# Both MLP products of an encoder block by Strassen's algorithm, with activations and residual rows passed through DRAM

## The chip, the cores and the metric

The kernel runs on one core of a Trainium2 chip. The metric is device time in microseconds of one execution; three runs of the kernel before have a median of 2367.69 us. The profile is one execution on the chip, and its times are in microseconds from the first instruction. The engines are TensorE (PE; its weight loads are PEld), VectorE (DVE), ScalarE (ACT), GpSimd (POOL) and SyncE (SP), which here only issues transfers.

## The reference

One layer of a streaming encoder for 512 tokens of width 2048, in f32: a norm, an input projection, latent attention and sparse attention side by side, an output projection, cross attention to 256 memory tokens, and then the part that this case is about:

```python
        x = x + memory_cross_attention(hc, mem_n, ...)     # ends with the product by w_o_cross
        hm = rmsnorm(x, g_mlp[l])
        x = x + jnp.square(jax.nn.relu(hm @ w_up[l])) @ w_down[l]     # 2048 -> 8192 -> 2048
    return rmsnorm(x, g_final)
```

## The kernel before

Activations lie feature-major: a tile has 128 features on the partitions and the 512 tokens along the free axis. Each f32 operand of a product is taken apart into two float32r halves, hi and lo, and a product of two tiles is three matmuls into the same PSUM bank: hi x hi, hi x lo, lo x hi (`fmm3`, matmuls at L292).

The program is one stream of *units*. A unit is a block of weights, 128 x 1024 f32 (512 KB), with the products made from it. `loader` sends its DMA on SyncE's queue into one of three `wraw` buffers, `splitter` takes it apart (`hi_lo`: ScalarE casts the block to `whi`, VectorE subtracts, `wlo = wraw - whi`), three units ahead at most, and `unit.pe` issues the matmuls. All instructions of ScalarE, VectorE and GpSimd go through a helper at L134, so the profile gives that line for nearly all of them; they are told apart by tile and shape. The order of each engine's instructions is settled while the program is written out: background tasks (Python generators) yield the time at which they can go on, and a plan with a clock for each engine (`Plan`, `Planned._cost`) decides when a task's next instruction is given to its engine. On the chip each engine runs its own list in order and waits at its head.

The MLP goes through the 8192 hidden features in eight chunks `c`. For a chunk, 16 up units make eight tiles of 128 hidden features: 16 contraction tiles, each product 128 x 512 into one of eight banks. When a bank is complete, `relu2` multiplies it by the tokens' norm `bc` (VectorE), applies relu and square (VectorE) and splits it into two `slot` tiles `A2` (ScalarE, VectorE). Then 16 down units multiply these tiles and `add_down` adds each finished bank to the residual `res[n]`, which stays on chip all along. The last eight down units (`last_units`) keep their weights on chip and run over the tokens in two halves of 256, so that the first half's final norm and store (`gen_out`) lie beside the second half's products. Ahead of the MLP, the eight units of `w_oc` finish the cross attention; `residual` adds each bank to the residual, writes its gained halves `NEWX` and sums its squares on GpSimd.

Matmuls of the MLP before: 248 units of 24 over 512 columns, and 8 units of 48 over 256 columns.

## Time and profile before

| what | value |
|---|---|
| median of three runs | 2367.69 us (2367.07 to 2368.04) |
| span of the profiled execution | 2365.2 us |
| TensorE busy in it | 2329.9 us, 99% |
| VectorE, ScalarE, GpSimd busy | 1123.1, 744.5, 173.0 us |
| moved by DMA | 234.91 MB, mean 99 GB/s |

The span runs from the first to the last instruction; the run's time contains it and some 2.5 us around it. A matmul's record is longer than the distance to the next one's start, because matmuls are pipelined: the pace is read from start to start, not from the record's length. Records of VectorE overlap a little in the same way.

### The profile page before, as it was taken

The numbers are of one execution on the slowest core, as the hardware profiler recorded it, in microseconds if no ns is written. First come the engines' busy times: TensorE is split into PE (matmuls) and PEld (weight loads), VectorE is DVE, ScalarE is ACT, GpSimd is POOL, SyncE is SP. The second block draws the span as 40 slices with busy tenths as digits, with TensorE's granted clock in tenths as the row PEclk, the third lists the DMA queues.
The fourth block names the chain that finished last, engine by engine and source line by source line (L and its number), as shares of the span: only waits on it lengthen the run. The fifth ranks groups of instructions, "written<-read, shape, count | busy, mean of one in ns | idle before, by whom it ended". The sixth has DMA issues, their size and how long they took to land.

```text
span 2365.2 us, 28572 instructions
## 1 busy us (share of the span) xinstructions
PE 2329.9 (99%) x11608; PEld 2020.0 (85%) x11608; DVE 1123.1 (47%) x1769; ACT 744.5 (31%) x1145; POOL 173.0 (7%) x232
## 2 busy tenths in 40 slices
...
GB/s 171 102 87 94 67 78 84 65 108 40 92 165 96 169 113 120 91 97 98 98 98 98 98 93 95 97 98 98 98 98 96 93 96 98 98 98 98 98 96 92
DMA packets 74406, 234.91 MB, mean 99 GB/s; under 512 B 8193, under 2 KB 12305, under 8 KB 74017
## 3 DMA queue, kind: packets, MB, share of 16 engines
...
## 4 chain that ended last, share of the span: by engine, by line
PE 59%; DVE 0%; POOL 0%; issue 0%; DVEq 0%; ACT 0%; POOLq 0%; ACTq 0%
PE bank L292 59%; DVE fb L134 0%; POOL fb L134 0%; PE bank L311 0%; DVEq L1719 0%; ACT fb L134 0%; POOL small L134 0%; POOLq L134 0%; ACTq L134 0%
## 5 line engine op out<-in xcount | busy, mean ns | idle before, releaser
L292 PE MATMUL bank<-slot,whi 128*128 128x512 f32 x4452 | 1382.3, 389 | 0.0
L134 DVE TENSOR_TENSOR wlo<-wraw,whi 128x1024 fp32r<-128x1024 f32 (+4 forms) x434 | 502.7, 1158 | 1064.9 <-ACT whi L134 1063.9
L292 PEld LDWEIGHTS bank<-slot,whi 128*128 128x128 f32 x4452 | 834.9, 188 | 171.5
L292 PE MATMUL bank<-slot,wlo 128*128 128x512 f32 x2268 | 883.2, 389 | 0.0
L134 ACT CAST whi<-wraw 128x1024 fp32r<-128x1024 f32 (+4 forms) x434 | 427.6, 985 | 1289.3 <-PE bank L292 1249.4
L292 PEld LDWEIGHTS bank<-slot,wlo 128*128 128x128 f32 x2268 | 425.8, 188 | 87.8
L292 PE MATMUL bank<-whi,slot 128*128 128x384 f32 (+4 forms) x1944 | 487.9, 329 | 7.4 <-ACT slot L134 6.9
L292 PEld LDWEIGHTS bank<-whi,slot 128*128 128x128 f32 x1944 | 343.5, 189 | 14.5 <-ACT slot L134 6.9
L292 PE MATMUL bank<-wlo,slot 128*128 128x384 f32 (+4 forms) x972 | 319.3, 329 | 0.5 <-DVE wlo L134 0.5
L134 POOL TENSOR_TENSOR fb<-fb 128x512 f32<-128x512 f32 (+5 forms) x118 | 108.3, 928 | 1668.9 <-issue 1348.2
L292 PEld LDWEIGHTS bank<-wlo,slot 128*128 128x128 f32 x972 | 184.0, 189 | 4.2 <-DVE wlo L134 0.9
L134 DVE TENSOR_TENSOR fb<-fb,bank 128x512 f32<-128x512 f32 (+1 forms) x192 | 122.5, 640 | 63.2 <-PE bank L292 61.8
L292 PE MATMUL bank<-slot,slot 128*128 128x256 f32 (+2 forms) x677 | 127.9, 311 | 0.6 <-DVE ptb L134 0.4
L292 PE MATMUL bank<-ptb,whi 128*128 128x512 f32 x380 | 123.8, 389 | 0.0
L292 PEld LDWEIGHTS bank<-slot,slot 128*128 128x128 f32 x677 | 103.3, 190 | 6.6 <-DVE slot L134 0.9
L292 PEld LDWEIGHTS bank<-ptb,whi 128*128 128x128 f32 x380 | 71.3, 188 | 14.8
L134 ACT CAST slot<-fb 128x512 fp32r<-128x512 f32 x75 | 46.2, 621 | 73.7 <-DVE fb L134 73.6
L311 PE MATMUL bank<-cs,fb 128*128 128x128 f32 x384 | 60.2, 275 | 9.0 <-POOL fb L134 3.6
L292 PE MATMUL bank<-ptb,slot 128*128 128x256 f32 (+1 forms) x323 | 65.3, 308 | 1.5 <-ACT slot L134 0.9
L134 DVE SCALAR_TENSOR_TENSOR slot<-fb,gn,slot 128x512 fp32r<-128x512 f32 (+1 forms) x75 | 65.4, 896 | 1.1 <-ACT slot L134 0.7
L134 ACT ACTIVATE fb<-fb 128x512 f32<-128x512 f32 (+2 forms) x94 | 51.1, 551 | 39.0 <-DVE fb L134 34.8
L311 PEld LDWEIGHTS bank<-cs,fb 128*128 128x128 f32 x384 | 46.3, 140 | 17.3 <-POOL fb L134 5.8
...
## 6 DMA issues: line engine op xcount, KB each, us to landing
wraw<-in_w_up_dram SPq DMA_DIRECT2D x128, 512.0 KB, 3.3
wraw<-in_w_dn_dram SPq DMA_DIRECT2D x128, 512.0 KB, 3.3
...
wraw<-in_w_out_dram SPq DMA_DIRECT2D x32, 512.0 KB, 3.3
fb<-in_xT_dram SPq DMA_DIRECT2D x16, 256.0 KB, 4.2
wraw<-in_w_in_dram SPq DMA_DIRECT2D x16, 256.0 KB, 2.6
fb<-in_xT_dram SPq DMA_DIRECT2D x8, 512.0 KB, 6.0
fb<-in_memT_dram SPq DMA_DIRECT2D x16, 256.0 KB, 3.1
```

What stands on the lines that cost most here:

```text
L134: r = fn(*args, **kw)
L292: nc.tensor.matmul(out, lhsT, rhs, start=start, stop=stop)
L311: nc.tensor.transpose(out, in_, ident)
```

## The change

The up and the down product are each cut into blocks of two by two (features, contraction, and token halves of 256) and made by the form of Strassen's algorithm with seven block products in place of eight. What goes with it:

- `strassen_split`: a unit's weights are four blocks of 256 columns. GpSimd forms four sums of them into a ring of two buffers (`sring`), then three blocks as they are (768 columns) and the four sums (1024 columns) are cast and subtracted into one of two buffers `HI`, `LO`.
- `strassen_pe`: a unit makes seven products of 256 columns for two feature halves `e`, three matmuls each. Seven banks stay open over the eight units of a group; the eighth is free.
- For the right-hand side four sums are needed too. `gen_xpair` makes them once for the eight pairs of input tiles, on VectorE for the first two pairs and on GpSimd for the others, and keeps pairs in `big`. For the hidden activations, `gen_up_out` combines the seven banks of an up group into four blocks (`c11`, `c21`, `c12`, `c22`), applies relu, square and the squared norm, forms the sums and both halves (`HT`, `G`), and ScalarE's queue stores them to `tp_dram`.
- All 16 up groups (8 units each) run first, then 16 down groups: four contraction quarters `c`, four output groups `ng`. `gen_load_t` loads the pairs of a quarter on ScalarE's queue into the place of a pair whose last product is issued.
- `residual1` stores the residual rows to `xs_dram`; `gen_load_res` loads them, on SyncE's queue, into the space of `G`, `HT` and `CT` when the last up group has been stored. `gen_down_out` adds the seven banks of a down group to them, the parts on PSUM by VectorE, the others by GpSimd (by VectorE for the last group).
- The two-half end is gone: `gen_square` sums squares by group, and `gen_out` scales and stores all 16 tiles after the last product.
- The plan has other costs for the MLP, and some buffers share one tile.

```diff
...
-    whi = [cp.tile([128, 1024], F32R, name=f"whi{i}") for i in range(3)]
-    wlo = [cp.tile([128, 1024], F32R, name=f"wlo{i}") for i in range(3)]
...
+    hl = cp.tile([128, 2 * PAIR], F32R, name="hl")
+    whi = [hl[:, 2048 * i : 2048 * i + 1024] for i in range(3)]
+    wlo = [hl[:, 2048 * i + 1024 : 2048 * i + 2048] for i in range(3)]
...
+    xs_dram = nc.dram_tensor("xs_dram", (KT, 128, 512), F32, kind="Internal").ap()
+    tp_dram = nc.dram_tensor("tp_dram", (32, 128, PAIR), F32, kind="Internal").ap()
...
+    def smm(out, lhsT, rhs, start, stop):
+        nc.tensor.matmul(out, lhsT, rhs, start=start, stop=stop, skip_group_check=True)
+        plan.issue("pe", 13.4 + rhs.shape[-1] / 2.4, [out], [lhsT, rhs], 30)
+        step()
...
                             fmm3(st[i], w_block(h, l, j, i), koper(k), k == 0, k == nk - 1)
                         if kk == nk // 2 - 1:
-                            spawn(residual(phase, 4 * ng + i, st[i], gain), True)
...
+    def residual1(n, b):
+        yield rt(b, res[n])
+        dve.tensor_tensor(res[n], res[n], b, op=OP.add)
+        banks_f.put(b)
+        flag.add(("x1", n))
+        if n % 2:
+            spawn(gen_xpair(n // 2), True)
+        yield rt(res[n])
+        nc.sync.dma_start(xs_dram[n], res[n])
+        while n > 0 and ("sq", 1, n - 1) not in flag:
+            yield 0
+        if n == 0:
+            act.activation(acc_r, res[n], AF.Square)
+        else:
+            act.activation(sq_r[n % 2], res[n], AF.Square)
+            yield rt(sq_r[n % 2])
+            pool.tensor_tensor(acc_r, acc_r, sq_r[n % 2], op=OP.add)
+        flag.add(("sq", 1, n))
+    def sums(dst, b12, b11, b21, b22, eng):
+        t1, t2, t3, t4 = dst
+        eng.tensor_tensor(t3, b22, b12, op=OP.subtract)
+        eng.tensor_tensor(t1, b12, b11, op=OP.subtract)
+        eng.tensor_tensor(t2, t3, b11, op=OP.add)
+        eng.tensor_tensor(t4, t2, b21, op=OP.subtract)
+    def gen_xpair(q):
+        while ("x1", 2 * q) not in flag or ("x1", 2 * q + 1) not in flag:
+            yield 0
+        gx = (yield from take(gxbufs))[0]
+        x1, x2 = res[2 * q], res[2 * q + 1]
+        g1, g2 = (g_mlp[:, 2 * q + j : 2 * q + j + 1] for j in range(2))
+        yield rt(x1, x2)
+        act.activation(gx[:, 0:256], x1[:, 256:512], AF.Copy, scale=g1)
+        act.activation(gx[:, 512:1024], x2, AF.Copy, scale=g2)
+        act.activation(gx[:, 256:512], x1[:, 0:256], AF.Copy, scale=g1)
+        yield rt(gx)
+        c = lambda i: gx[:, 256 * i : 256 * i + 256]
+        sums([c(4), c(5), c(6), c(7)], c(0), c(1), c(2), c(3), dve if q < 2 else pool)
+        pr = yield from take_pair(q)
+        for a, n in ((0, 768), (768, 1024)):
+            src = gx[:, 256 + a : 256 + a + n]
+            yield from hi_lo(pr[:, a : a + n], pr[:, 1792 + a : 1792 + a + n], src)
+        gxbufs.put(gx)
+        XP[q] = pr
+        flag.add(("xp", q))
+        if q == 3:
+            while not all(("sq", 1, n) in flag for n in range(8)):
+                yield 0
+            gxbufs.put(fslot(6144, 2048))
...
+    def strassen_split(i):
+        raw, s = wraw[i % 3], sring[i % 2]
+        hi, lo = HI[units[i].buf], LO[units[i].buf]
+        while i == first_s and not all(("xp", q) in flag and ("sq", 1, 2 * q + 1) in flag for q in range(2)):
+            yield 0
+        while not splits[i - 2].done:
+            yield 0
+        yield rt(raw)
+        two = lambda x: x.rearrange("p (u c) -> p u c", u=2)
+        a21 = raw[:, 0:256]
+        pool.tensor_tensor(two(s[:, 0:512]), two(raw[:, 256:768]), a21.unsqueeze(1).to_broadcast([128, 2, 256]), op=OP.add)
+        pool.tensor_tensor(s[:, 512:768], s[:, 256:512], raw[:, 256:512], op=OP.add)
+        pool.tensor_tensor(s[:, 768:1024], s[:, 512:768], raw[:, 768:1024], op=OP.add)
+        while ("pe", i - 2) not in flag:
+            yield 0
+        yield from hi_lo(hi[:, 0:768], lo[:, 0:768], raw[:, 256:1024])
+        yield from hi_lo(hi[:, 768:1792], lo[:, 768:1792], s)
+    def strassen_pe(buf, st, pair, first, last, order):
+        hi, lo = HI[buf], LO[buf]
+        for r in order:
+            w, t = PRODUCTS[r]
+            if first:
+                st[r] = take_now(banks_f)[0]
+            th, tl = pair[:, 256 * t : 256 * t + 256], pair[:, 1792 + 256 * t : 2048 + 256 * t]
+            for e in range(2):
+                out = st[r][:, 256 * e : 256 * e + 256]
+                c = part(256 * w + 128 * e)
+                smm(out, hi[:, c], th, first and e == 0, False)
+                smm(out, hi[:, c], tl, False, False)
+                smm(out, lo[:, c], th, False, last)
+    G = fslot(0, 4096)
+    HT = fb[:, 6144 : 6144 + 3584].bitcast(F32R)
+    CT = fslot(10496, 2048)
...
+    def gen_up_out(g, st):
+        e1, e5, u2, u3 = (G[:, 2048 + 512 * i : 2560 + 512 * i] for i in range(4))
+        c11, c21, c12, c22 = (CT[:, 512 * i : 512 * i + 512] for i in range(4))
+        while g == 0 and len(gxbufs) < 2:
+            yield 0
+        while g > 0 and ("t", g - 1) not in flag:
+            yield 0
+        yield rt(st["p1"])
+        act.copy(e1, st["p1"])
+        banks_f.put(st["p1"])
+        yield rt(e1, st["p2"])
+        dve.tensor_tensor(c11, e1, st["p2"], op=OP.add)
+        banks_f.put(st["p2"])
+        yield rt(st["q5"])
+        act.copy(e5, st["q5"])
+        banks_f.put(st["q5"])
+        yield rt(st["q6"])
+        dve.tensor_tensor(u2, e1, st["q6"], op=OP.subtract)
+        banks_f.put(st["q6"])
+        dve.tensor_tensor(u3, u2, st["p7"], op=OP.add)
+        banks_f.put(st["p7"])
+        dve.scalar_tensor_tensor(c21, st["q4"], -1.0, u3, op0=OP.mult, op1=OP.subtract)
...
+        banks_f.put(st["q4"])
+        yield rt(st["p3"])
+        dve.tensor_tensor(c12, u2, st["p3"], op=OP.add)
+        banks_f.put(st["p3"])
+        dve.tensor_tensor(c22, e5, u3, op=OP.subtract)
+        dve.tensor_tensor(c12, c12, e5, op=OP.subtract)
         while "bc" not in flag:
             yield 0
...
+        four = lambda x: x.rearrange("p (m e c) -> p m e c", m=2, e=2)
+        blocks = G.rearrange("p (b m c) -> p b m c", b=8, m=2)
+        for t, src in ((0, CT[:, 0:1024]), (1, CT[:, 1024:2048])):
+            yield rt(src)
+            act.activation(src, src, AF.Relu)
...
+            yield rt(src)
+            d = blocks[:, 1:3] if t == 0 else blocks[:, 0:4:3]
+            d = d.rearrange("p b m c -> p m b c")
+            act.activation(d, four(src), AF.Square)
+            yield rt(d)
+            b = bc[:, 256 * t : 256 * t + 256].unsqueeze(1).unsqueeze(1).to_broadcast([128, 2, 2, 256])
+            dve.tensor_tensor(d, d, b, op=OP.mult)
+        c = lambda i: G[:, 512 * i : 512 * i + 512]
+        yield rt(G[:, 0:2048])
+        sums([c(4), c(5), c(6), c(7)], c(0), c(1), c(2), c(3), dve)
+        for a in (0, 1792):
+            src = G[:, 512 + a : 2304 + a]
+            yield from hi_lo(HT[:, a : a + 1792], src.bitcast(F32R), src)
+        for x, o in ((HT.bitcast(F32), 0), (G[:, 512:4096], 1792)):
+            yield rt(x)
+            for m in range(2):
+                dst = tp_dram[2 * g + 1 - m][:, o : o + 1792].rearrange("p (r c) -> p r c", r=7)
+                nc.scalar.dma_start(dst, x.rearrange("p (r m c) -> p r m c", r=7, m=2)[:, :, m, :])
+        flag.add(("t", g))
...
+            def run(buf):
+                if g == 0 and kk == 0:
+                    spawn(gen_rstd_l())
+                until(lambda: kk in XP)
+                strassen_pe(buf, st, XP[kk], kk == 0, kk == 7, ORDER)
+                if kk == 7:
+                    spawn(gen_up_out(g, st), True)
+                if g == 15:
+                    spawn(gen_load_t(kk))
+            return run
...
+    def gen_load_t(p):
+        yield plan.clk["pe"]
+        while ("t", p // 2) not in flag:
+            yield 0
+        dst = big[:, PAIR * (p % 8) : PAIR * (p % 8) + PAIR]
+        nc.scalar.dma_start(dst.bitcast(F32), tp_dram[p])
+        plan.issue("dma", 100.0, [dst], [], 7000)
+        TP[p] = dst
+    CB = [[[fslot(o + 1024 * m + 512 * t) for t in range(2)] for m in range(2)]
...
+    def gen_load_res():
+        while ("t", 15) not in flag:
+            yield 0
+        for ng in range(4):
+            for m in range(2):
+                for t in range(2):
+                    dst = CB[ng][m][t]
+                    n = 4 * ng + 2 * (1 - m)
+                    src = xs_dram[n : n + 2, :, 256 * t : 256 * t + 256].rearrange("e p c -> p e c")
+                    nc.sync.dma_start(dst.rearrange("p (e c) -> p e c", e=2), src)
+                    plan.issue("dma", 100.0, [dst], [], 3000)
+            flag.add(("res", ng))
...
+    def gen_down_out(c, ng, st, last):
+        (c11, c12), (c21, c22) = CB[ng]
+        while ("res", ng) not in flag:
+            yield 0
+        e1, u2, u3 = yield from take(ev, 3)
+        side = dve if last else pool
+        yield rt(st["p1"])
+        act.copy(e1, st["p1"])
+        banks_f.put(st["p1"])
+        def add(dst, r, op, free=True):
+            dve.tensor_tensor(dst, dst, st[r], op=op)
+            if free:
+                banks_f.put(st[r])
...
+        else:
+            yield rt(st["p2"], e1)
+            add(c11, "p2", OP.add)
+            side.tensor_tensor(c11, c11, e1, op=OP.add)
+            yield rt(st["q5"])
+            add(c12, "q5", OP.subtract, False)
+            add(c22, "q5", OP.add)
+            yield rt(st["q6"])
+            dve.tensor_tensor(u2, e1, st["q6"], op=OP.subtract)
+            banks_f.put(st["q6"])
+            dve.tensor_tensor(u3, u2, st["p7"], op=OP.add)
+            banks_f.put(st["p7"])
+            add(c21, "q4", OP.subtract)
+            yield rt(st["p3"])
+            add(c12, "p3", OP.add)
+            side.tensor_tensor(c12, c12, u2, op=OP.add)
+            side.tensor_tensor(c21, c21, u3, op=OP.subtract)
+            side.tensor_tensor(c22, c22, u3, op=OP.subtract)
...
+            def run(buf):
+                p = 8 * c + j
+                if c == 0 and ng == 0 and j == 0:
+                    spawn(gen_load_res())
+                until(lambda: p in TP)
+                order = LAST_ORDER if end and j == 7 else ORDER
+                strassen_pe(buf, st, TP[p], j == 0, j == 7, order)
+                if j == 7:
+                    if c == 3:
+                        for k in [x for x in flag if x[0] == "fin" and x[1] == ng]:
+                            flag.discard(k)
+                        spawn(gen_square(ng), True)
+                    spawn(gen_down_out(c, ng, st, end), True)
+                if ng == 3 and c < 3:
+                    spawn(gen_load_t(p + 8))
+            return run
...
+    def gen_out():
+        rs = rstd_l
+        b = (yield from take(banks_f))[0]
+        yield rt(acc_f)
+        for tb in range(4):
+            mm(b[:, 2 * tb : 2 * tb + 2], blk(acc_f, tb), ones, True, True)
+        yield rt(b)
+        rsqrt_mean(rs, b[:, 0:8:2], D)
         banks_f.put(b)
...
+            for m in range(2):
+                for e in range(2):
+                    n = 4 * ng + 2 * (1 - m) + e
+                    v = tile_view(ng, m, e)
+                    if (ng, m, e) in gained:
+                        pool.tensor_tensor(v, v, b2, op=OP.mult)
+                        q = nc.scalar
...
+                        dve.scalar_tensor_tensor(v, v, g_fin[:, n : n + 1], b2, op0=OP.mult, op1=OP.mult)
+                        q = nc.sync
+                    q.dma_start(outT[128 * n : 128 * n + 128, :].rearrange("p (u c) -> p u c", u=2), v)
+                    yield 0
...
@@ -1563,14 +1828,16 @@
                 slots.put(*t)
     units.extend(proj_units(1, w_oc, 4, OC.get, g_mlp, oc_hook))
-    for c in range(8):
-        units.extend(up_units(c))
...
+    first_s = len(units)
+    for g in range(16):
+        units.extend(up_units(g))
+    for c in range(4):
+        for ng in range(4):
+            units.extend(down_units(c, ng))
+    for i, u in enumerate(units):
+        u.buf = (i - first_s) % 2 if i >= first_s else (i - first_s) % 3
...
-            yield from u.own(i)
+        if i >= first_s:
+            yield from strassen_split(i)
         elif u.src is not None:
             n = u.n
-            yield from hi_lo(whi[i % 3][:, 0:n], wlo[i % 3][:, 0:n], wraw[i % 3][:, 0:n])
+            yield from hi_lo(whi[u.buf][:, 0:n], wlo[u.buf][:, 0:n], wraw[i % 3][:, 0:n])
...
```

## Rows read from the trace of the kernel before

**Rows 1.** The page, part 1: busy us, share, instructions
```profile
span 2365.2 us, 28572 instructions
...
PE 2329.9 (99%) x11608; PEld 2020.0 (85%) x11608; DVE 1123.1 (47%) x1769; ACT 744.5 (31%) x1145; POOL 173.0 (7%) x232
```

**Rows 2.** MLP stretch: busy us (instructions) by engine, clock, DMA share, GB/s
```profile
1000.00:1200.00 200.00, 200.00 (x885) 165.58 (x883) 72.65 (x80) 43.80 (x46) 0.00 (x0) 1.00 0.29 98
```

**Rows 3.** TensorE's timeline near the end: start us, us, instructions merged
```profile
2290.04 0.62 PE L292 MATMUL bank<-slot,whi 128*128 128x512 f32 x2
...
2301.37 0.39 PE L292 MATMUL bank<-slot,wlo 128*128 128x512 f32 x1
2301.60 3.15 PE L292 MATMUL bank<-slot,slot 128*128 128x256 f32 x25
2304.59 0.28 PE L292 MATMUL bank<-ptb,slot 128*128 128x256 f32 x1
...
2347.95 0.52 PE L292 MATMUL bank<-ptb,slot 128*128 128x256 f32 x3
```

**Rows 4.** Groups from 1000 us on: busy us, mean ns, idle before
```profile
L134 DVE TENSOR_TENSOR wlo<-wraw,whi 128x1024 fp32r<-128x1024 f32 x238 | 291.5, 1225 | 759.8 <-ACT whi L134 759.8
L134 ACT CAST whi<-wraw 128x1024 fp32r<-128x1024 f32 x237 | 249.8, 1054 | 925.8 <-PE bank L292 925.8
...
L292 PEld LDWEIGHTS bank<-slot,slot 128*128 128x128 f32 x256 | 35.4, 192 | 0.1
...
L134 POOL TENSOR_TENSOR fb<-fb 128x256 f32<-128x256 f32 x33 | 26.2, 798 | 1367.8 <-issue 1348.2 <-ACT fb L134 18.1
```

**Rows 5.** VectorE's timeline inside the MLP, GpSimd idle
```profile
1209.22 1.22 DVE L134 TENSOR_TENSOR wlo<-wraw,whi 128x1024 fp32r<-128x1024 f32 x1 [4.21 <-ACT whi L134]
1210.36 0.68 DVE L134 TENSOR_TENSOR fb<-bank,fb 128x512 f32<-128x512 f32 x1
1211.08 0.69 DVE L134 SCALAR_TENSOR_TENSOR fb<-fb 128x512 f32<-128x512 f32 x1
...
1213.02 0.69 DVE L134 TENSOR_TENSOR slot<-fb,slot 128x512 fp32r<-128x512 f32 x1
1213.62 0.68 DVE L134 TENSOR_TENSOR fb<-bank,fb 128x512 f32<-128x512 f32 x1
```

**Rows 6.** VectorE's timeline before the MLP, GpSimd at work
```profile
928.66 0.67 DVE L134 TENSOR_TENSOR fb<-fb,bank 128x512 f32<-128x512 f32 x1
...
930.37 2.31 DVE L134 TENSOR_TENSOR wlo<-wraw,whi 128x1024 fp32r<-128x1024 f32 x1
932.60 1.77 DVE L134 SCALAR_TENSOR_TENSOR slot<-fb,gn,slot 128x512 fp32r<-128x512 f32 x1
```

**Rows 7.** GpSimd's timeline over the same microseconds
```profile
926.89 3.01 POOL L134 TENSOR_TENSOR fb<-fb 128x512 f32<-128x512 f32 x2 [3.81 <-ACT fb L134]
930.12 3.71 POOL L134 TENSOR_TENSOR fb<-fb 128x512 f32<-128x512 f32 x2 [0.22 <-ACT fb L134]
```

**Rows 8.** DMA issues by line: count, KB each, median us from issue to landing
```profile
wraw<-in_w_up_dram SPq DMA_DIRECT2D x128, 512.0 KB, 3.3
...
out_dram<-fb SPq DMA_DIRECT2D x12, 256.0 KB, 2.2
```

**Rows 9.** Stretches with the DMA engines full, at the start
```profile
5.00:10.00 5.00, 3.15 (x9) 2.69 (x10) 3.04 (x4) 3.85 (x7) 0.00 (x0) 1.00 0.98 355
10.00:15.00 5.00, 5.00 (x24) 5.00 (x23) 4.08 (x5) 5.00 (x9) 1.58 (x2) 1.00 0.94 312
```

**Rows 10.** Timeline of the tail, all engines
```profile
2349.81 0.42 DVE L134 TENSOR_TENSOR fb<-fb 128x256 f32<-128x256 f32 x1 [0.88 <-POOL fb L134]
...
2353.30 6.87 DVE L134 SCALAR_TENSOR_TENSOR fb<-fb,gn 128x256 f32<-128x256 f32 x11 [1.97 <-ACT fb L134]
2353.34 4.17 POOL L134 TENSOR_TENSOR fb<-fb 128x256 f32<-128x256 f32 x5 [1.23 <-ACT fb L134]
2355.24 4.95 ACTq L1453 DMA_DIRECT2D out_dram<-fb  x4
```

312 lines of the change are left out of this document (154 added, 158 removed).

## The prediction

> **What bounds the kernel now.** I read the engines' totals first: TensorE is busy 99% of a 2365.2 us span [rows 1]. The three runs have a median of 2367.7 us, 2.5 us above that span; I work in the span and add the 2.5 at the end. The stretches of the MLP say the same from inside: in 200 us TensorE is busy 200, VectorE 73, ScalarE 44, GpSimd nothing, and the DMA engines 0.29 at 98 GB/s [rows 2]. So in the MLP only TensorE sets the time, and the other engines are free cover, which the change spends.
>
> The pace comes from TensorE's timeline. Between 2290.04 and 2301.37 us fifty products of 512 columns start, 226.6 ns each. From 2301.60 us, where the last units run on token halves, 25 products of 256 columns take 2.99 us, 119.6 ns each, and that stretch ends near 2348.3 us [rows 3]. The MLP before has 248 units of 24 wide products and 384 narrow ones: 5952 x 0.2266 + 46.7 = 1395 us, 43.5 us for each 8 units.
>
> **Products.** Each of the 256 units now makes seven block products x two feature halves x three split terms = 42 products of 256 columns. All weights still change at every product, as in the narrow stretch before, which is why I take its 119.6 ns. 256 x 42 x 0.1196 = 1286 us, 40.2 us for 8 units. The gain is 109 us, not the eighth that the column count promises (174), because a narrow product costs 53% of a wide one. If nothing else became late, the span would be 2256 us.
>
> The Trainium skill (TensorE: Matmul & The Clock Gate, Back-to-back issue gap) gives 262 cycles for 256 columns and 518 for 512, an estimate of 109 and 216 ns at 2.4 GHz. By it the gain would be near 153 us. The rows disagree at both widths (119.6 and 226.6), so the measurement decides.
>
> **VectorE and GpSimd.** Per unit, the split before was a 1024-wide cast on ScalarE (1054 ns) and a 1024-wide subtract on VectorE (1225 ns) [rows 4]. Now GpSimd first makes four block sums (512 + 256 + 256 wide), and cast and subtract run over 768 and 1024. On VectorE start to start, 1024 columns cost 1.14 us, 512 cost 0.60, and an instruction that needs the one before it 0.72 [rows 5]; hence 0.87 for 768, 1.95 for 1792, 2.0 per unit. GpSimd needs 1.5 us for 512 [rows 7] and 0.8 for 256 [rows 4], so 3.1 per unit of 5.03.
>
> After each up group of 8 units come five VectorE operations on a PSUM and an SBUF operand (3.4 us), and ten on two SBUF operands: two subtractions for c22 and c12 (1.3), two multiplications by the squared norm (2.3), four sums (2.6), two subtracts of 1792 (3.9), together 10.1.
>
> The critical row is an old one. While GpSimd works, VectorE's 1024-wide subtract of two SBUF operands takes 2.31 us instead of 1.22, its successor starts after 2.23 instead of 1.14, and a 512-wide one takes 1.77; an addition with one operand in PSUM keeps its 0.67 [rows 5, 6]. GpSimd's two additions in that overlap take 3.71 instead of 3.01 [rows 7]. So VectorE's two-operand work runs at half speed under GpSimd, and GpSimd at some 0.8. The Trainium skill (GPSIMD Engine Reference, Specifications) says that the two share SBUF interfaces and names VectorE instructions with two SBUF inputs as a case of contention; the trace agrees, with 2.31 against 1.22 us. It speaks against this change, which wakes GpSimd in just the stage where it slept.
>
> Count a unit of an up group on VectorE. A split's sums wait for the second subtract two units earlier (two buffers), so that subtract, 1.14 us, is uncontended. GpSimd then works 3.3 us, in which VectorE gets 1.7 of its remaining 0.87 + 10.1/8 = 2.13 us done. The other 0.43 and the PSUM work, 3.4/8 = 0.43, follow: 1.14 + 3.3 + 0.43 + 0.43 = 5.3 us against TensorE's 5.03, so 42.4 us a group without idling. I take 43, since VectorE sometimes waits for ScalarE's cast: 2.8 us too many for 15 groups, +42. Below stands 40.2 (all covered), above 47 (next paragraph). ScalarE has 1.9 us of casts per unit and about 9 per group, 24 of 40, and isn't the bound. In the down groups VectorE has 16 us of subtracts and seven PSUM additions (4.6), GpSimd 25 + 6 of additions; with the contention 31 and 36 of 40.2, so I charge 5 us for all of down, mainly the last quarter, where the squares' sums are added to GpSimd.
>
> **The way through DRAM.** An up group writes 3.67 MB from buffers of which there is one set. The next group's first evacuation (ScalarE's copy of p1 into the same buffer) waits until these stores have read it. Behind that copy on ScalarE stand the casts of the next units, and TensorE waits for p1's bank at its second product. From p1's copy: evacuation 5.4 us, relu, square and multiply 6.5, sums 3.5, casts and subtracts 7, and 8 us for the unit splits in between: 30. The stores start some 5 us before that end. The DMA engines at 0.94 to 0.98 busy moved 312 to 355 GB/s [rows 9] and weights take 0.29 of them, which leaves about 230 GB/s, 8 us per half, and landing after a store of 256 KB takes 2.2 in all [rows 8]. So the ring closes after about 30 + 8 + 2 = 40 us, just under 43. If VectorE's share in it is contended throughout, add 6 to 7 us: 47.
>
> **From up to down.** In the last up group the loads of the first eight activation pairs (1.84 MB each, one per 5 us, 364 GB/s) enter ScalarE's DMA queue ahead of group 14's stores. At 230 GB/s the queue is some 4 MB behind when the stores arrive; group 15's evacuation waits, and TensorE with it, about 20 us. Then SyncE's queue: the 16 residual loads (4.2 MB) wait at its head for the last stores, and the next weights, which land in 3.3 us now [rows 8], stand behind them: about 8 us more. Together +28; 8 if the loads drain at 355 GB/s, 50 if both stalls come in full. Later quarters have 35 us from the first free buffer to its need; nothing is charged.
>
> **Ends.** From w_oc to up, pairs form in about 9 us each on one buffer, while TensorE asks for one every 5 us and the fourth is ready near the start: +2. The tail loses its two-half overlap. Before, the last sum on VectorE (2349.81) is followed by the first scaled tile at 2353.30 and the last stores at 2355 to 2365 [rows 10]. Now all 16 tiles follow the last product: 4.2 MB at 330 GB/s are 13 us after 6 of norm, against 17 from the last product before: +2 to +8, +5 taken.
>
> **Sum.** 2365.2 - 109 + 42 + 5 + 28 + 2 + 5 = 2338, plus 2.5 is 2340 us.
>
> **Rivals.** First, TensorE stays the bound: GpSimd and VectorE interleave in their free gaps, up groups take 40.2 to 40.5 and the switch 10 to 20 us. For it: VectorE's own work is 29.6 us of the 40.2, so contention has to cost it 11 before it is full. Against it: GpSimd is busy two thirds of each unit. 2365.2 - 109 + 15 for the switch + 15 for up, down and the ends + 2.5 = 2289 us. Chance 0.25.
>
> Second, and on the other side: the single set of up buffers closes its ring at 47 us. Place: ScalarE's copy of p1 behind the stores, every group. Price: 6.8 x 15 = 102 instead of 42, so 2400 us. It decides from 44.8 us on, where 15 x 4.6 eats what is left of the 109 after the other 40. For it: the ring's estimate is already as long as the group. Against it: while TensorE stalls, GpSimd and the splits pause, and the evacuation runs uncontended. Chance 0.29.
>
> Third, the change doesn't buy its products: a narrow product whose weight load isn't hidden. Weight loads of the narrow stretch average 192 ns and yet its products start every 119.6 ns for 46 us [rows 3, 4], so it gets 0.02.
>
> **Numbers.** The likeliest, VectorE-bound up groups, has 0.44 and its own range is 2312 to 2368. Its upper end lies within 0.2% of before (4.7 us, about what a measurement of this kernel can tell from no change): 0.04 of it, and the third rival's 0.02, make 0.06 for no change. Faster: the first rival's 0.25 and the other 0.40 of the likeliest, 0.65; slower: the second rival's 0.29. The range takes in the first rival nearly to its floor and most of the second: 2278 to 2415 us.
>
> **What the profile would show.** Right: 119 to 121 ns from narrow product to narrow product inside a unit; the 1024-wide subtract between 1.22 and 2.31 us; in up stretches TensorE with gaps of 2 to 3 us per group at a bank that waits for ScalarE or VectorE, VectorE over 90% busy, GpSimd near 65%; in down stretches TensorE full; one break of 20 to 30 us between up and down with ScalarE or SyncE's queue waiting for stores. Wrong: up groups of 40.3 us (first rival), or group starts at which p1's copy waits for DMA for 5 us and more (second). An up group whose units stall evenly, with no group-start gap, would mean that GpSimd's sums, not VectorE, are late.

## The result, and the profile after

The changed kernel takes 2441.19 us (median of four runs, 2439.85 to 2445.15) beside 2367.85 us for the kernel before: a ratio of 1.0314, interval 1.0299 to 1.0329. It is slower, by 73 us; 2340 us had been forecast. The profiled execution has a span of 2438.0 us.

The page's first part, which answers to [rows 1]: the chip issues more products (16,024) in less time of TensorE, and GpSimd's 173 us have become 1385.

```profile
span 2438.0 us, 39899 instructions
...
PE 2275.2 (93%) x16024; PEld 2182.4 (90%) x16024; DVE 1683.8 (69%) x2018; ACT 1056.9 (43%) x1481; POOL 1385.2 (57%) x1078
```

Two stretches of 200 us, the first in the up groups, the second in the down groups, with the columns of [rows 2]:

```profile
1000.00:1200.00 200.00, 185.12 (x1514) 183.30 (x1513) 173.60 (x138) 100.55 (x107) 165.12 (x110) 0.99 0.50 169
1800.00:2000.00 200.00, 197.54 (x1626) 196.62 (x1625) 135.04 (x112) 72.54 (x83) 188.60 (x136) 0.99 0.48 175
```

In the up groups no engine is full on average: TensorE 93%, VectorE 87%, GpSimd 83%. The groups of instructions of the up stretch (1000 to 1560 us), beside [rows 4], show what the operations cost now:

```profile
L139 POOL TENSOR_TENSOR fb<-fb,wraw 128x256 f32<-128x256 f32 x199 | 274.6, 1380 | 15.6
L139 POOL TENSOR_TENSOR fb<-wraw 128x512 f32<-128x512 f32 x100 | 177.8, 1778 | 92.5 <-DVE hl L139 85.5 <-DMA wraw<-in_w_up_dram 6.9
L139 DVE TENSOR_TENSOR hl<-fb,hl 128x1024 fp32r<-128x1024 f32 x100 | 153.4, 1534 | 68.9 <-ACT hl L139 62.1 <-PE bank L310 6.8
L139 DVE TENSOR_TENSOR hl<-wraw,hl 128x768 fp32r<-128x768 f32 x100 | 136.4, 1364 | 2.7 <-ACT hl L139 2.5
L139 ACT CAST hl<-fb 128x1024 fp32r<-128x1024 f32 x99 | 103.7, 1048 | 156.9 <-POOL fb L139 124.5 <-PE bank L310 21.4 <-issue 3.7
...
L139 DVE TENSOR_TENSOR fb<-fb,bank 128x512 f32<-128x512 f32 x49 | 33.3, 680 | 1.6 <-PE bank L310 1.1
```

GpSimd's three sums of a unit take 1.78 + 2 x 1.38 = 4.5 us here, not the 3.1 (3.3 beside VectorE) of the prediction. VectorE's 1024-wide subtract takes 1.53 instead of 1.22 [rows 5]; its additions from PSUM keep their 0.68. The idle times form a ring: VectorE's subtracts wait 62.1 + 2.5 us for ScalarE's casts, the casts 124.5 for GpSimd's sums, and the sums 85.5 for VectorE's subtracts, which free the two buffers of sums.

An average hides where the time goes inside a group. TensorE's timeline of one up group (it starts at 1334.7 us; the first row begins with the window) has two breaks, both for VectorE's half of a split:

```profile
1332.81 17.44 PE L310 MATMUL bank<-big,hl 128*128 128x256 f32 x144
1351.83 5.30 PE L310 MATMUL bank<-big,hl 128*128 128x256 f32 x42 [1.58 <-DVE hl L139]
1359.33 16.94 PE L310 MATMUL bank<-big,hl 128*128 128x256 f32 x139 [2.20 <-DVE hl L139]
```

Inside a stretch the pace is the predicted one: 144 products in 17.44 us, less the 0.28 of the last record, are 120 ns each. The other groups look alike: by TensorE's starts, groups 2 to 15 lose 1.9 us each in their fourth unit, 3.0 in their fifth, and next to nothing in the other six. In windows of 10 us, VectorE (third busy figure) is full for 30 us and then has a third of its time free; TensorE loses its time in the second and third window:

```profile
1332.00:1342.00 10.00, 10.00 (x86) 10.00 (x85) 9.92 (x12) 7.79 (x9) 8.00 (x6) 1.00 0.27 99
1342.00:1352.00 10.00, 8.42 (x70) 8.22 (x70) 9.97 (x9) 4.95 (x5) 6.88 (x6) 1.00 0.17 52
1352.00:1362.00 10.00, 7.80 (x64) 7.60 (x65) 10.00 (x7) 4.65 (x6) 7.69 (x4) 1.00 0.94 308
1362.00:1372.00 10.00, 10.00 (x85) 10.00 (x85) 6.58 (x5) 3.45 (x5) 9.46 (x8) 1.00 0.81 280
```

What VectorE does there is the *late work* of the group before: the four sums and the two subtracts of 1792 columns that turn its hidden activations into operands. It stands between the splits that TensorE waits for (VectorE's timeline):

```profile
1346.23 4.68 DVE L139 TENSOR_TENSOR fb<-fb 128x512 f32<-128x512 f32 x4
1350.83 0.94 DVE L139 TENSOR_TENSOR hl<-wraw,hl 128x768 fp32r<-128x768 f32 x1
1351.70 1.21 DVE L139 TENSOR_TENSOR hl<-fb,hl 128x1024 fp32r<-128x1024 f32 x1
1352.84 5.04 DVE L139 TENSOR_TENSOR fb<-fb 128x1792 fp32r<-128x1792 f32 x2
1357.80 1.47 DVE L139 TENSOR_TENSOR hl<-wraw,hl 128x768 fp32r<-128x768 f32 x1
```

**Where the time went, by group.** From TensorE's starts I took the length of each of the 32 groups (16 up, 16 down), from its first product to that of the next group, in the profiled execution; 40.2 us is a group at 119.6 ns per product. Groups 16 to 18 are the switch from up to down, groups 21, 25 and 29 start a contraction quarter, "steady" is the mean of the other down groups from 19 to 28, and the tail runs from the last product to the end. The table has all runs but e8, which holds no layer.

```
run                  time     group 1  2-15    16, 17, 18        steady  21, 25, 29        30, 31, 32        tail
                     us                 mean                      down
changed kernel       2441.19  69.6     45.28   48.5 56.2 47.0    40.4    45.2 46.9 46.6    47.3 48.1 47.7    28.8
e1 no sums           2306.97  51.4     40.32   48.2 53.6 43.3    40.3    40.5 41.5 40.7    40.3 40.3 40.3    28.9
e2 sums on VectorE   2430.92  60.2     44.37   47.8 52.1 52.8    42.8    49.4 51.7 48.1    41.6 42.1 42.1    28.9
e3 no late work      2392.12  69.5     41.87   45.4 60.7 42.4    40.4    48.2 46.3 47.3    47.3 48.2 47.7    28.8
e4 small pieces      2458.25  69.6     46.38   47.3 50.3 51.8    40.4    47.1 46.6 48.1    44.6 50.6 48.2    29.2
e5 sums unread       2459.79  69.2     45.89   48.1 61.5 45.7    41.2    47.2 45.4 42.5    52.2 48.1 47.5    29.0
e6 residual spread   2428.07  69.0     45.39   48.6 48.2 40.3    40.4    46.4 45.6 48.6    44.6 50.5 48.2    28.8
e7 mixed             2547.92  64.1     49.74   55.0 50.7 42.9    46.9    47.3 46.0 46.8    47.4 47.9 47.8    27.7
e9 no mult           2430.91  68.5     43.55   43.5 52.3 55.4    41.5    50.5 48.1 46.6    44.6 50.6 48.2    28.8
e10 moved            2402.62  60.3     45.41   49.7 47.8 40.3    40.4    45.8 47.2 46.6    43.0 41.9 42.3    27.6
e11 both             2380.34  60.4     43.08   44.7 43.8 47.1    41.7    47.6 48.1 46.6    41.6 41.9 42.3    28.0
e12 spread loads     2356.39  60.4     42.98   43.3 46.7 50.1    40.4    41.0 41.7 42.2    43.0 41.9 42.3    27.6
e15 e12 again        2360.23  60.4     43.28   43.9 44.9 50.8    40.3    41.2 41.7 41.7    43.0 41.9 42.3    27.6
e13 spread late      2404.14  58.9     45.46   50.4 44.5 59.0    40.3    40.8 41.4 41.6    43.0 42.0 42.3    27.6
e14 tail from PSUM   2404.42  60.4     45.56   50.8 43.5 59.1    40.3    40.4 41.6 41.0    43.0 41.9 42.2    27.7
e16 late, short gaps 2354.43  60.2     42.73   43.7 45.3 51.9    40.4    41.1 41.7 41.8    43.0 41.9 42.2    27.6
e17 late subtract    2346.97  58.9     42.14   43.2 45.7 53.9    40.4    40.5 41.7 42.2    43.0 41.9 42.3    27.6
```

Over the 32 x 40.2 us of bare products the changed kernel has 29 us in the first group, 71 in groups 2 to 15, 31 where up turns into down (16 to 18), 18 at the starts of the contraction quarters (21, 25, 29), 23 in the last three and 2 elsewhere: 174 us. Before, the MLP took 1398.5 us from its first product to its last; it takes 1460.4 now. That is 62 of the 73 us; the tail after the last product, 28.8 us against 16.9, is the rest.

The switch, in SyncE's timeline: the 16 residual loads stand in one row, the next weights behind them, and in the window there TensorE idles and its granted clock falls to 0.50 (1.2 GHz) after the break.

```profile
1729.23 18.74 SPq L1586 DMA_DIRECT2D fb<-xs_dram  x16
1748.38 15.87 SPq L423 DMA_DIRECT2D wraw<-in_w_dn_dram  x5
```
```profile
1745.00:1755.00 10.00, 4.01 (x34) 3.81 (x32) 0.00 (x0) 0.00 (x0) 0.00 (x0) 0.92 1.08 371
1755.00:1765.00 10.00, 5.49 (x20) 4.59 (x21) 5.64 (x7) 4.17 (x6) 8.66 (x7) 0.50 0.36 118
```

### The profile page after: what moved, and what is told of

Read it like the earlier page. It is cut to its first block, busy times and chain, and to the rows that moved or that the text cites. A ratio compares the mean times of both kernels' runs of the same rounds, so it can differ in the third digit from the quotient of the medians.

```text
span 2438.0 us, 39899 instructions
## 1 busy us (share of the span) xinstructions
PE 2275.2 (93%) x16024; PEld 2182.4 (90%) x16024; DVE 1683.8 (69%) x2018; ACT 1056.9 (43%) x1481; POOL 1385.2 (57%) x1078
## 4 chain that ended last, share of the span: by engine, by line
PE 45%; POOL 26%; DVE 14%; issue 8%; DMA 5%; ACT 1%; SPq 0%; DVEq 0%; ACTq 0%; POOLq 0%
PE bank L305 30%; POOL fb L139 26%; PE bank L310 14%; DVE fb L139 8%; DVE hl L139 4%; DMA wraw<-in_w_dn_dram 4%; PE bank L330 2%; DVE big L139 1%; DMA wraw<-in_w_up_dram 1%; ACT hl L139 0%; POOL acc_f L139 0%; DMA tp_dram<-fb 0%; DMA fb<-xs_dram 0%; ACT fb L139 0%; DVE small L139 0%
## 5 line engine op out<-in xcount | busy, mean ns | idle before, releaser
L310 PE MATMUL bank<-big,hl 128*128 128x256 f32 x10752 | 1339.1, 287 | 103.0 <-DVE hl L139 73.4
L310 PEld LDWEIGHTS bank<-big,hl 128*128 128x128 f32 x10752 | 1323.3, 196 | 118.4 <-DVE hl L139 84.3
L139 DVE TENSOR_TENSOR hl<-wraw,hl 128x768 fp32r<-128x768 f32 (+4 forms) x442 | 568.6, 1287 | 330.8 <-ACT hl L139 329.8
L139 POOL TENSOR_TENSOR fb<-fb,wraw 128x256 f32<-128x256 f32 x512 | 671.9, 1312 | 40.1
L139 DVE TENSOR_TENSOR hl<-fb,hl 128x1024 fp32r<-128x1024 f32 x256 | 390.1, 1524 | 297.2 <-ACT hl L139 278.4
L139 ACT CAST hl<-wraw 128x768 fp32r<-128x768 f32 (+4 forms) x442 | 378.9, 858 | 464.9 <-PE bank L305 289.8
L305 PE MATMUL bank<-hl,big 128*128 128x384 f32 (+4 forms) x2916 | 525.0, 330 | 7.5 <-ACT big L139 6.5
L139 POOL TENSOR_TENSOR fb<-wraw 128x512 f32<-128x512 f32 x256 | 414.7, 1620 | 171.6 <-DVE hl L139 117.8
L305 PEld LDWEIGHTS bank<-hl,big 128*128 128x128 f32 x2916 | 479.2, 189 | 18.5 <-ACT big L139 6.5
L305 PE MATMUL bank<-big,hl 128*128 128x512 f32 (+1 forms) x1192 | 296.1, 390 | 0.0
L305 PEld LDWEIGHTS bank<-big,hl 128*128 128x128 f32 x1192 | 222.2, 188 | 43.3
```

What stands on the lines that cost most here:

```text
L139: r = fn(*args, **kw)
L305: nc.tensor.matmul(out, lhsT, rhs, start=start, stop=stop)
L310: nc.tensor.matmul(out, lhsT, rhs, start=start, stop=stop, skip_group_check=True)
```

## The experiments

The first four ask what the up groups wait for. Theory A: GpSimd's sums. Theory B: VectorE's late work, which stands ahead of the splits in its order.

**e1, no sums.** The second cast and subtract read the raw weights.

```diff
-        pool.tensor_tensor(two(s[:, 0:512]), ...)        # and the two of 256
-        yield from hi_lo(hi[:, 768:1792], lo[:, 768:1792], s)
+        yield from hi_lo(hi[:, 768:1792], lo[:, 768:1792], raw)
```

> Leaves out GpSimd's three block-sum instructions of every MLP unit (the second cast and subtract read the raw weights instead, same widths); VectorE's, ScalarE's and TensorE's work is unchanged. Theory A, GpSimd's sums are the cause (slow, and sharing with VectorE): up groups 1 to 14 fall from 45.3 to 40.3-41.5 us, the first group from 69.6 to under 55, down groups 29 to 31 from 47.7 to under 43; time near 2310 us (2290 to 2340). Theory B, VectorE's up work blocks the unit splits in its in-order queue, whoever makes the sums: up groups stay at 44 us or more and only the last quarter gains; time 2400 or more.

2306.97 us. Up groups 40.32, quarter starts and last groups near 40.3 too. Without the sums nothing but the first group, the switch and the tail is left of the loss. VectorE in groups 2 to 15, in the changed kernel and here:

```profile
1018.35:1652.24 633.89, 582.18 (x4707) 576.30 (x4706) 552.49 (x436) 321.29 (x336) 507.21 (x337) 0.98 0.52 175
1000.60:1565.10 564.50, 564.50 (x4706) 564.50 (x4705) 419.11 (x435) 319.91 (x336) 0.00 (x0) 1.00 0.57 196
```

That is 39.5 us busy and 5.8 idle per group with the sums, and 29.9 busy for the same instructions without them: GpSimd's work lengthens VectorE's by 9.6 us a group.

**e2, the sums on VectorE,** at the same place in the program, ahead of the splits.

```diff
-        pool.tensor_tensor(s[:, 512:768], s[:, 256:512], raw[:, 256:512], op=OP.add)     # all three
+        dve.tensor_tensor(s[:, 512:768], s[:, 256:512], raw[:, 256:512], op=OP.add)
```

> The same block sums on VectorE instead of GpSimd: some 1.35 us more per unit on VectorE, nothing on GpSimd in the units. Theory A with contention as the main part: VectorE has 40 us of uncontended work per up group and runs just full, up groups 42 to 43.5, down groups 40.3, last quarter 41 to 42, first group 50 to 58; time 2345 to 2375. If not sharing but the amount of elementwise work counts (B): VectorE, now with 11 us more per group, is later than before, up groups 48 or more, time above 2450.

2430.92 us: up groups 44.4, between the two ranges, so neither theory is met. VectorE is busy 186 us of 200 in the up stretch, so it has no room for the sums either. The run is some 10 us faster than with the sums on GpSimd. By the prediction's own count its work per up group is 29.5 us; the three sums take 1.46 us by themselves (e8), so 29.5 + 8 x 1.46 = 41.2 before any wait.

**e3, no late work.** The four sums, casts and subtracts of the hidden activations are left out of the up groups; the stores stay, with the same bytes.

```diff
-        sums([c(4), c(5), c(6), c(7)], c(0), c(1), c(2), c(3), dve)
-            yield from hi_lo(HT[:, a : a + 1792], src.bitcast(F32R), src)
```

> Leaves out, in each up group, the four sums, the two 1792-wide casts and the two 1792-wide subtracts of the activations (VectorE 6.5 us uncontended, 9.7 in the trace; ScalarE 3.4), and stores the upper part twice; GpSimd's block sums stay. Theory A says that GpSimd alone already is short of time: its unit loop takes 4.3 us of 5.03 and is not bound, so only the VectorE part counts: up groups 41 to 42.5, first group, quarter starts and last quarter unchanged; time 2385 to 2405. Theory B: up groups 40.3, time near 2370. If the ring through DRAM counted, the same stores would keep the groups at 44 or more.

2392.12 us, up groups 41.87, as A said; the stores alone don't hold the groups at 44. **e4, the same work in small pieces:**

```diff
-        for a in (0, 1792):
+        for a in range(0, 3584, 512):            # and a yield behind each of the four sums
```

> Same work, but the activations' sums are given to VectorE one by one and their halves are made in seven pieces of 512 columns instead of two of 1792, so that no VectorE instruction of the up groups lasts longer than about 1.2 us and the unit splits come in between. Theory B (blocking at the head of VectorE's queue): up groups fall from 45.3 to 41-43, time 2385 to 2415. Theory A (rate, not order): up groups within 1 us of 45.3, time 2430 to 2455.

2458.25 us, up groups 46.38, just outside both ranges and nowhere near B's 41 to 43; TensorE's loss moved to the sixth unit of a group. So far A came nearer in all but e2; it fell with the next run.

**e5, sums that nobody reads.** GpSimd works as in the changed kernel, but the second split reads `raw`.

```diff
-        yield from hi_lo(hi[:, 768:1792], lo[:, 768:1792], s)
+        yield from hi_lo(hi[:, 768:1792], lo[:, 768:1792], raw)
```

> GpSimd makes every unit's block sums as in the changed kernel, but nobody reads them: the second cast and subtract read the raw weights, so four of seven products have the wrong operand (only the time counts). Theory A (lateness: the casts wait for sums that come too late): the up groups 2 to 15 fall to 40.3 to 41.0 us and the run to 2305 to 2330 us, as with no sums at all. Theory C (slowdown: GpSimd's traffic lengthens VectorE's own operations until VectorE sets the pace): nothing is gained by not reading them, up groups 43 to 45 us, run 2375 to 2420 us.

2459.79 us, up groups 45.89: not faster than with sums that are waited for, and above C's 43 to 45. Beside e1, whose second split reads `raw` as well, only the unread sums are new, and they cost 5.6 us a group. The groups of the same stretch show where:

```profile
L139 DVE TENSOR_TENSOR hl<-wraw,hl 128x1024 fp32r<-128x1024 f32 x98 | 170.6, 1741 | 30.3 <-ACT hl L139 30.0
...
L139 DVE TENSOR_TENSOR fb<-fb 128x1024 f32<-128x1024 f32 x24 | 43.4, 1807 | 0.0
```

VectorE no longer waits for the sums' cast as long (30 us for 69), and its subtracts are longer instead (1.74 for 1.53). A, in the sense that the sums come late, is refuted for the up groups: it is that they are being made. Theory C takes its place: the two engines slow each other, and VectorE's slowed work sets the pace. The test isn't quite clean, because `raw` is now held until the second subtract, and GpSimd waits 123.9 us of the 560 for weights (6.9 in the changed kernel). TensorE's own waits name VectorE alone, 48.0 us.

**e8, the disputed operations alone,** stage after stage on made-up data, in windows of one stage each (behind the length VectorE, ScalarE, GpSimd):

> No layer at all, only the disputed operations by themselves on made-up data, stage after stage: VectorE's subtract of 1024 columns (two SBUF operands) alone, a unit's three sums on GpSimd alone, both together, VectorE's PSUM addition of 512 alone and with the sums, ScalarE's copy of 1024 with the sums, the three sums on VectorE. My reading of the changed kernel's trace: subtract 1.1 to 1.25 us alone and 1.5 to 2.3 beside the sums; sums 2.8 to 3.0 us alone, 5 to 6.5 beside the subtracts (as both lose, the loss of both together is larger than either's work), 2.8 to 3.2 beside PSUM additions that take 0.67 either way, 2.8 to 3.0 beside ScalarE's copies. What my prediction used: sums 3.1 alone, 3.8 beside the subtracts, subtract at half speed. Rival (GpSimd's times here come from its dependent chain and its queue, not from VectorE): sums about 4.2 in every stage.

```profile
11.60:48.70 37.10, 36.35 (x35) 0.48 (x4) 1.07 (x2) 1.00 0.00 0
48.70:94.70 46.00, 0.39 (x2) 0.27 (x2) 42.99 (x50) 1.00 0.00 0
94.70:169.40 74.70, 57.72 (x35) 0.38 (x2) 71.67 (x50) 1.00 0.00 0
169.40:198.80 29.40, 28.88 (x51) 0.38 (x2) 0.40 (x3) 1.00 0.00 0
198.80:244.90 46.10, 28.55 (x51) 0.47 (x3) 43.12 (x51) 1.00 0.00 0
244.90:290.90 46.00, 0.43 (x2) 30.49 (x34) 43.03 (x50) 1.00 0.00 0
290.90:315.90 25.00, 23.38 (x51) 0.43 (x3) 0.54 (x2) 1.00 0.09 33
315.90:352.90 37.00, 36.22 (x34) 30.62 (x34) 1.08 (x2) 1.00 0.05 19
```

First 32 subtracts of 1024 alone (36.4 us), then 16 units' sums alone (43.0), then both: 57.7 and 71.7. Next VectorE's 48 additions from PSUM, alone and beside the sums: 28.9 and 28.6, and the sums keep their 43. ScalarE's copies (sixth line) don't touch the sums either, and the last line has them beside the subtracts, which keep their 36.2. The line above it is VectorE making the 16 units' sums itself: 23.4 us. In the third stage, while both work:

```profile
L248 DVE TENSOR_TENSOR fb<-fb 128x1024 f32<-128x1024 f32 x19 | 33.8, 1854 | 0.0
L256 POOL TENSOR_TENSOR fb<-wraw 128x512 f32<-128x512 f32 x6 | 13.4, 2241 | 0.0
L257 POOL TENSOR_TENSOR fb<-fb,wraw 128x256 f32<-128x256 f32 x6 | 9.5, 1584 | 0.5
L258 POOL TENSOR_TENSOR fb<-fb,wraw 128x256 f32<-128x256 f32 x6 | 9.5, 1583 | 0.5
```

A subtract goes from 1.21 to 1.85 us, a unit's sums from 43.0 / 16 = 2.7 to 2.24 + 2 x 1.58 = 5.4. Handing the 16 units to GpSimd lengthened VectorE's own work by 21.4 us, nearly as much as the 23.4 of doing them itself, and the last of them were made after VectorE had ended. By 5.4 us a unit, an estimate, only 10.7 of the 16 units lie beside VectorE's 57.7 us, so each cost it 2.0 us, more than the 1.46 of making it. Side by side the two jobs took 71.7 us; one after the other they would take 36.4 + 43.0 = 79.4. The rival (a slow chain on GpSimd, whatever VectorE does) is refuted.

**e9, less work on VectorE in the up groups.** The activations' two multiplications by the squared rstd are taken out; the residual is divided by it once, in the down groups.

```diff
-            dve.tensor_tensor(d, d, b, op=OP.mult)            # gen_up_out, twice a group
+        if c == 0:                                            # gen_down_out, four tiles
+            dve.tensor_tensor(v, v, inv[:, 256 * t : 256 * t + 256]..., op=OP.mult)
```

> Computes the whole result. The two multiplications of an up group's activations by the squared rstd (128x1024, 1.49 us each on VectorE in the changed kernel's up groups) are left out of the up groups; instead the residual is divided by it once, in the first four down groups (16 multiplications of 128x512), and the closing rstd takes the factor in. Theory C (VectorE, slowed by GpSimd, sets the pace of the up groups): 3.0 us less on VectorE, up groups 42.0 to 43.5 us instead of 45.3, run 2400 to 2418 us. Rival (the pace is set by waits in the order of work, a cast for its sums or a split behind the late work): up groups 44.6 to 45.3 us, run 2430 to 2442 us.

Up groups 43.55, where C said 42.0 to 43.5 and the rival 44.6 to 45.3. VectorE was busy 4.6 us a group less (34.9 for 39.5), and the group became only 1.7 shorter: its total isn't all that sets the pace. The run, 2430.91, lies in the rival's range: the 16 multiplications stand at the end of groups 17 to 20, which took 197.5 us for 184.0.

**e6, the residual's loads spread out,** the weights' loads between them.

```diff
                     plan.issue("dma", 100.0, [dst], [], 3000)
+                    yield plan.clk["pe"] + 1500               # gen_load_res; 9000 ahead of the first
```

> The changed kernel with only the 16 loads of the residual delayed and spread out behind the weights on SyncE's queue. If the 16 loads in one row on that queue hold up the down units' first weights (my reading of the switch), the three groups at the switch fall from 151.7 us to 135 to 143, and the run to 2424 to 2434 us. Rival (the switch waits for VectorE or for the stores of the last up groups): 148 to 152 us, and the run stays at 2438 to 2444.

2428.07 us, switch 137.1: as my reading said. **e7, sums shared out,** on top of e6: in up groups 2 to 16 the 512-wide one on GpSimd and the others on VectorE between its two subtracts, elsewhere all three there; the tail's multiplications on VectorE too.

```diff
         yield from hi_lo(hi[:, 0:768], lo[:, 0:768], raw[:, 256:1024])
+        dve.tensor_tensor(s[:, 512:768], s[:, 256:512], raw[:, 256:512], op=OP.add)     # and the next
```

> Computes the whole result. First block sum (512 columns) on GpSimd in up units after the first group, all other sums on VectorE behind its first subtract, residual loads spread, the tail's multiplications on VectorE alone. Theory A: up groups 40.5 to 42, down groups 41 to 43 (VectorE near its limit), switch about 140, run 2340 to 2375 us. Theory C: VectorE, which now does 0.96 us more in each unit, sets the pace everywhere: up groups 43 to 45, run 2395 to 2430 us.

2547.92 us, beyond both. By the order of the program the sums, ScalarE's cast and the second subtract now follow one another behind the first subtract; that TensorE waits for this whole chain is argued, not tried, and the run doesn't tell the theories apart.

**e10, four pieces moved from GpSimd to VectorE,** on top of e6.

```diff
-        sums(..., dve if q < 2 else pool)                     # gen_xpair
+        sums(..., dve)
-        side = dve if last else pool                          # gen_down_out
+        side = dve if c == 3 else pool
-            eng = dve if ng == 3 else pool                    # gen_square
+            eng = dve
-                        pool.tensor_tensor(v, v, b2, op=OP.mult)          # gen_out
+                        dve.tensor_tensor(v, v, b2, op=OP.mult)
```

> Computes the whole result. The changed kernel with the residual's loads spread (as before), and four pieces of GpSimd's work on VectorE: the x pairs' sums before and in the first group, the last quarter's additions, its sums of squares, and the six multiplications of the tail. Theory: GpSimd's queue is what the first group, the last quarter and the tail wait for: first group 69.6 us to 56 to 63, the last three groups 47.7 to 41 to 44 each, tail 28.8 to 25 to 27, switch 137 as in the run before, up groups unchanged at 45.3; run 2390 to 2412 us. Rival (what GpSimd sheds VectorE picks up and is late in its place): first group over 66, last groups 46 and more, run 2420 to 2432 us.

2402.62 us; first group 60.3, last groups 42 to 43, as the theory said; the tail, 27.6, missed its 25 to 27. **e11, e9 and e10 together,** with the fifth product of an up group read from PSUM by VectorE in place of a copy:

> Computes the whole result. The two edits before together, and the up groups read the fifth product from PSUM instead of a copy of it. If both theories hold: first group 56 to 63, up groups 41.5 to 43, switch 133 to 140, down 40.4, last groups 41 to 44, tail 25 to 27; run 2350 to 2380 us, near the kernel before's. If VectorE's time is not what the up groups wait for: 2390 to 2412.

2380.34 us, at the edge of its range; up groups 43.08, switch 135.6, but the tail (28.0) and the down groups (41.7 on average, with e9's multiplications in them) didn't follow. **e12, loads spread:** pair loads of a new quarter start 1.6 us later each, the residual's multiplications move to the middle of a group.

```diff
-        yield plan.clk["pe"]
+        yield plan.clk["pe"] + (1600 * (p % 8) if p >= 8 else 0)     # gen_load_t
```

> Run e11 with two things spread out: the loads of the next chunk's activation pairs (1.8 MB each) start 1.6 us later each from the second on, and the residual's 16 multiplications run in the middle of a group, 2.5 us apart, not at a group's end. If the quarter starts (47.6, 48.1, 46.6 us in e11) wait for weights that share the DMA engines with those loads (share 1.0 and 420 GB/s there), they fall to 40.3 to 42; rival (GpSimd is late by its own work): 46 to 48. Groups 17 to 20, where the multiplications stood at the end: 43.8, 47.1, 44.3, 47.4 us to 40.3 to 42.5. Run 2380 us to 2348 to 2362; by the rival 2364 to 2374.

2356.39 us. The quarter starts fell from 47 to 41 or 42: the weights had come late while the pair loads filled the DMA engines. Groups 17 and 18, forecast at 40.3 to 42.5 with the multiplications moved, rose instead to 46.7 and 50.1; why isn't shown. In e11, ahead of group 25, GpSimd's timeline names the wait and the window the load:

```profile
1994.23 1.29 POOL L139 TENSOR_TENSOR fb<-wraw 128x512 f32<-128x512 f32 x1 [2.81 <-DMA wraw<-in_w_dn_dram]
```
```profile
1990.00:2000.00 10.00, 10.00 (x85) 10.00 (x85) 4.47 (x4) 3.15 (x4) 4.91 (x6) 1.00 1.01 427
```

**e13, e12 with the late work in eight pieces at least 2 us apart; e14, the same with the tail's factor read from PSUM by VectorE, and the six multiplications back on GpSimd.**

```diff
             dve.tensor_tensor(o, x, y, op=op)                 # e13, each of the four sums
+            yield plan.clk["pe"] + 2000                       # and behind each 896 columns of the split
-  dve.scalar_tensor_tensor(v, v, g_fin[:, n : n + 1], b2, op0=OP.mult, op1=OP.mult)     # e14
+  dve.scalar_tensor_tensor(v, v, g_fin[:, n : n + 1], b3, op0=OP.mult, op1=OP.mult)
```

> As e12, and the late work of an up group (four sums of 512 and the split of 3,584 columns) is issued in eight pieces at least 2 us apart. If the 1.9 us stall in each up group of e11 is a split behind the lump of late work, up groups fall from 43.1 to 40.4 to 41.5 us and the run by 22 to 36 us against e12; rival (VectorE's total time in a group sets the pace, as pieces alone changed nothing in e4): 42.6 to 43.5, and the run within 6 us of e12.

> As e13, but in the tail VectorE reads the closing factor from PSUM and GpSimd's six multiplications stay on GpSimd. If the tail's multiplications were slowed by the two engines' shared way to SBUF, and a PSUM operand takes VectorE off it as in e8, VectorE's ten take 0.68 us each and GpSimd's six 1.3 us each, both side by side: 8 us instead of 11 to 13, tail 28.0 to 22.5 to 25. If not, the tail stays at 27 to 29.

Both expectations failed. e13 took 2404.14 us, up groups 45.5, slower than either range. Its breaks now stand mostly in the first unit of a group (3.7 us): the late work ends so late that ScalarE's copy of p1 waits for the stores of the group before, in each of 14 groups (1010 to 1650 us, in total, times, longest):

```profile
ACT fb L139 <- DMA tp_dram<-fb: 61.2, 14, 5.8
```

e14 made the multiplications as fast as expected and left the tail at 27.7. VectorE's timeline, GpSimd's, and a window after both had ended:

```profile
2386.60 6.67 DVE L139 SCALAR_TENSOR_TENSOR fb<-fb,gn,bank 128x512 f32<-128x512 f32 x10 [2.92 <-ACT fb L139]
```
```profile
2386.64 7.39 POOL L139 TENSOR_TENSOR fb<-fb 128x512 f32<-128x512 f32 x6 [1.87 <-ACT fb L139]
```
```profile
2394.50:2396.50 2.00, 0.00 (x0) 0.00 (x0) 0.00 (x0) 0.00 (x0) 0.00 (x0) 0.50 1.03 340
```

Ten multiplications of 0.67 us and six of 1.23, where the changed kernel took 12.8 us for the ten. But the stores of the 4.2 MB output fill the DMA engines at 340 GB/s until the end: from its first store on the tail is bound by them.

**e16 and e17, e12 with the late work in eight pieces 0.3 and 0.7 us apart, or with its second split alone 1.5 us later; both start the residual's loads earlier. e15 is e12's kernel again.**

```diff
         for a in (0, 1792):
             src = G[:, 512 + a : 2304 + a]
+            yield plan.clk["pe"] + (1500 if a else 0)         # e17
             yield from hi_lo(HT[:, a : a + 1792], src.bitcast(F32R), src)
```

> As e12, with only the second subtract of 1,792 columns put 1.5 us later, behind the next unit's split, and the residual's loads as in e16. If the lump is what stalls the splits: up groups 40.8 to 42.2, run 2325 to 2345. Rival: 42.5 to 43.5, run 2345 to 2357.

> As e12, with the late work of an up group in eight pieces 0.3 and 0.7 us apart, done by the middle of the group, and the residual's loads and multiplications begun 6 us earlier and closer together. If the lump is what stalls the splits: up groups 40.4 to 41.8 (43.0 in e12), switch 125 to 135 (140.1), run 2318 to 2340. Rival (VectorE's total in that part of the group): up groups 42.5 to 43.5, run 2345 to 2357.

e15: 2360.23 us, ratio to the kernel before 0.9975 [0.9963, 0.9986]; its 12 runs lie between 2353.67 and 2368.02, so single runs of this kernel are good to some 7 us. e16: 2354.43 us, 0.9946 [0.9932, 0.9960], up groups 42.7: within e15's runs, and the rival's forecast. e17: 2346.97 us, 0.9917 [0.9904, 0.9930], up groups 42.1. e17 is the fastest version of the whole computation here: 0.8% under the kernel before. Its up groups are the lump's forecast, its time is 2 us above that range and in the rival's; the switch stayed long in both (141.0 and 142.9 us, 125 to 135 expected). Groups 2 to 15 of e12 and e17:

```profile
1010.20:1611.90 601.70, 574.60 (x4707) 568.92 (x4705) 483.14 (x407) 311.84 (x322) 487.15 (x337) 0.99 0.54 184
1009.80:1599.70 589.90, 572.15 (x4706) 566.06 (x4705) 500.05 (x408) 308.81 (x322) 503.48 (x337) 1.00 0.55 188
```

VectorE is busy longer in e17 (35.7 us a group for 34.5), and the group is shorter: here the order decided, not VectorE's total. Of the four tries at the lump (e4, e13, e16, e17) this one alone gained.

## Why the prediction was wrong

**Products: right.** The pace is 119.6 to 120 ns: steady down groups take 40.4 us, and nearly all groups of e1 40.3, against 40.2 of bare products. The third rival, a weight load that isn't hidden, is refuted by the same pace.

Of the 101 us by which the forecast fell short, the terms behind the products make up all (103; the gain on the products came out 3 larger, as the MLP before took 1398.5 and not 1395): down 37, up groups 29, first group 27, the tail 7, the switch 3.

**The step that failed first** is the count of a unit of an up group on VectorE: 42.4 us a group without idling, and 0.6 more because VectorE sometimes waits for ScalarE's cast; 43, +42. Measured: 45.28, +71. The contention that it names is the right cause (e1, e5, e8), and VectorE's work without it is right too (29.5 counted, 29.9 in e1). Its two other figures are not. First, I gave VectorE the larger loss, half its speed, and GpSimd only a fifth, from one pair of records [rows 6, 7] in which GpSimd overlapped VectorE for part of its time. Side by side for long (e8), VectorE loses a third and GpSimd half; so the sums take 4.2 to 4.5 us on average and up to 5.4. VectorE's busy time came out shorter than counted by it: 39.5 us a group, not 42.4 (87%, where over 90 was to be seen, and GpSimd 83%, not 65). Second, and this is what made the group longer, the wait that I put at 0.6 us measured 5.8: VectorE stands idle that long in each group, nearly all of it for a cast, and the casts mostly for GpSimd's slowed sums. It isn't the sums alone: in e5, where no cast waits for them, VectorE idles 5.0 us a group all the same, now for casts that wait until TensorE has freed a buffer of the split.

Behind the wait stands the order. I had spread the late work evenly over the group. It comes as a lump: VectorE is full for 30 us, then free for a third of the rest, and TensorE loses its 5 us in two places, the fourth and fifth unit, at a split and not, as I had said, at a bank. That the two-deep rings of splits and sums fail to bridge the lump is shown in part: moving one late split by 1.5 us (e17) won 0.8 us a group against e12 and 1.1 against e15, while cutting the lump into pieces (e4, e13, e16) won at most 0.3 against e12. The e12 group also had VectorE 5 us less busy (e9, e11), for 2.3 us of gain. How the last 1.9 us over 40.2 divide between order and VectorE's total stays open.

**First group, +2 forecast, +29 measured.** I counted the pairs' formation and not whose queue it stands in: GpSimd's, with squares' sums and unit sums behind it. e10, which moves the pairs' sums, takes 9 of the 29 off, e1 18. The other 11 stand without any sums (e1), against 2 forecast; what makes them isn't shown.

**Down, +5 forecast, +42 measured.** The steady groups are full, as forecast. The quarter starts, for which I charged nothing because the buffers come free in time, cost 18: I looked at the buffers and not at the weights that share the DMA engines with the loads (e12). The loads alone cost little: e1 has the same, and its quarter starts take 40.5 to 41.5. With the sums they cost 5 to 7 us each; that GpSimd, 94% busy in the down groups, can't catch up behind a late block of weights is my reading of the two runs. The last three groups cost 23: from 2060 us on a group's sums take GpSimd 8 x (1.45 + 2 x 1.24) = 31 us, its four additions 4 x 1.9 and its eight squares' sums 8 x 0.8, together 45 of 40.2 (e10 takes the last two away). Beside VectorE an addition that I had priced at 1.5 us takes 1.9.

**Switch, +28 forecast, +31 measured.** The size was right by luck. The part on SyncE's queue was there and larger (14.6 us went with e6, 8 were forecast); the 20 us on ScalarE's queue were not. The copy of p1 in group 16 goes without a wait:

```profile
1697.49 1.05 ACT L139 CAST hl<-fb 128x1024 fp32r<-128x1024 f32 x1 [2.76 <-POOL fb L139]
1698.45 0.58 ACT L139 COPY fb<-bank 128x512 f32<-128x512 f32 x1
```

The full DMA engines moved 408 to 427 GB/s there (1680 to 1700 us), not the 230 + 98 that I had allowed after [rows 9]; that the queue drained for this reason is argued, not tried. Something of that stall was there all the same: ScalarE stood for 9.3 us while its queue took 7.5 us to issue two stores, and group 16 took 48.5 us.

```profile
1675.37 7.54 ACTq L1542 DMA_DIRECT2D tp_dram<-fb  x2
1682.96 0.83 ACT L139 CAST hl<-wraw 128x768 fp32r<-128x768 f32 x1 [9.26 <-issue]
```

What makes the rest of the switch, some 16 us with e6's change in, stays open.

**Tail, +5 forecast, +12 measured.** The stores were priced rightly, 4.2 MB at 340 GB/s; the chain ahead of them was too short in my sum: 15 us pass between the last product and the first store's data (2409 to 2424), not 6 of norm. How to shorten that chain was not tried.

**The rivals.** The second rival's number (2400) came nearest and its mechanism is not what the changed kernel does: p1's copy waits for no store there, and e3, which keeps the stores, runs at 41.9. It is real all the same: in e13, where the late work ends later, that copy waits 4.4 us in each group. The first needed free gaps; VectorE has none for 30 us of a group.
